# Down projection of a gated feed-forward: from nine pairs of row blocks by seven products and a plain rest to eleven pairs by seven products

## The chip, the cores and the metric

One NeuronCore of a Trainium2 chip runs the whole kernel. The time is device microseconds of one execution, as the median of several runs; the profile is one more execution of the same program. TensorE (PE) multiplies, VectorE (DVE), ScalarE (ACT) and GpSimd (POOL) work on the results, and SyncE (SP) and ScalarE issue transfers (queue names SPq, ACTq).

## The reference

One decoder layer on 512 tokens of 1024 channels, float32. First comes a mixer (a matrix-memory head group and a convolution group) with a residual, then a gated feed-forward with a causal convolution of width 3 over the tokens. The change concerns the feed-forward alone:

```python
D_FF = ((8 * D_MODEL // 3 + 127) // 128) * 128      # 2816 = 22 blocks of 128
...
u = rms_norm(x, ffn_pre_g[l]) * (1.0 + sc2) + sh2
up = causal_dwconv(u @ ffn_up[l], ffn_conv_w[l], ffn_conv_b[l])
a, gt = jnp.split(up, 2, axis=-1)
f = (jax.nn.silu(gt) * a) @ ffn_down[l]
x = x + g2 * rms_norm(f, ffn_post_g[l])
```

## The kernel before

**Products of split numbers.** A float32 operand is split in two parts, `hi` (a copy in the TensorE's rounded format, made on ScalarE) and `lo` (the rest, by a subtraction on VectorE or GpSimd). `mm3` multiplies a pair of operands by three matmuls: hi by hi, hi by lo, lo by hi. `w_split` makes the two parts of a weight piece, `w_load` loads a megabyte of weights through SP and splits it in four.

**The up stage.** The loop `for i in range(NF)` goes over the 22 blocks of the hidden width. For block i TensorE computes 48 matmuls of 512 columns, 24 for the value half into one PSUM bank and 24 for the gate half into another (`mmbank`, a pool of four buffers, so that block i+2 writes the banks of block i). `conv3` reads each bank three times: ScalarE makes the first tap (L1027), VectorE adds two more (L1029). The results are `fa` and `fg`. ScalarE puts `fg` through silu in place (L1097); this instruction is the `anchor`. VectorE multiplies the two, by halves of 256 tokens: `fx` for the first half, `fr` for the second.

**The down stage by seven products.** Two neighbouring blocks make a pair. Of the product of hidden values and down weights, the token halves are the rows, the two blocks of the pair the inner halves and the two halves of 512 output channels the columns: a two by two product of blocks, which a scheme with sums of blocks does in seven products instead of eight. Its sums of hidden values (`fy`, `fq`) are made on GpSimd in the up stage at every odd block and split there, or sent to DRAM (`spill["s34"]`, `spill["a22"]`, through ScalarE's queue) and read back by `back` in the down stage. Its sums of weights are made in the up stage too, one pair at each block that the table `AT` lists: `weight_load` fetches the pair's four pieces `b` (256 KB each, through ScalarE's queue, put behind the last silu by `behind`), `weight_sums` does four subtractions (L1048 and L1050 on VectorE, L1049 and L1051 on GpSimd, in the order 1048, 1049, 1050, 1051, each after the one before), and `weight_store` sends the four results `spillt` to DRAM from ScalarE's queue, behind the silu of the block after the sums. In the down stage `product` fetches the weights of one of the seven products in pieces of `GJ` pairs through SP into a ring of four buffers, splits each pair's piece and does 6 matmuls per pair. The seven are p1, p2, p6, p5, p7, p3, p4 in this order. Eight PSUM banks (`banks`, four token tiles by two halves of the output channels) collect them; `keep` copies a finished sum out and `put` adds it into another bank.

**The rest and the end.** Nine pairs (blocks 0 to 17) go by seven products. Blocks 18 to 21 stay whole (`f`), and are multiplied by their weights `wd` plainly, token tile by token tile, 24 matmuls each. After each tile comes the end chain: the multiply by the gain into `fo` (L1205), squares of the bank summed on ScalarE (L678), the factor of the norm (`token_factor`, one small operation on VectorE, L683, and a power on GpSimd, L685), the last multiply with the residual `xr` added (L1210), and the output through SP (L1211).

**What sets the order.** TensorE's and SP's instructions run in the order in which the code is written. Those of VectorE, ScalarE and GpSimd are put in order by the compiler's list scheduler when the kernel is built; `behind` adds an edge to it. Each engine then works in order.

Of the kernel before, what the change touches and what calls it, by code (L numbers as in the profile page):

```python
# [17 lines left out]
P = 128  # L18
D = 1024
# [35 lines left out]
def decoder_layer(ctx, tc, w_glu0, x, c, adaT, vecs, w_glu, w_qko, w_v0, w_v, w_out, w_up, w_down, out):  # L55
# [32 lines left out]
    def slot(name, dt=F32):  # L88
        return slots.tile([P, T], dt, tag="t", name=name)
# [108 lines left out]
    def mm3(ps, a, b, start, stop, again=False):  # L198

        for i, (l, r) in enumerate(((a[0], b[0]), (a[0], b[1]), (a[1], b[0]))):  # L200
            PE.matmul(ps, l, r, start=start and i == 0, stop=stop and i == 2, skip_group_check=again)  # L201
# [471 lines left out]
    def cvtile(name):  # L673
        return cvs.tile([P, T], F32, tag="cvs", name=name)

    def sq_sum(src, col, name):
        junk = small.tile([P, T], BF16, tag="junk", bufs=1, name=f"{name}junk")
        S.activation(junk, src, AF.Square, accum_out=col)  # L678

    def token_factor(sq, name):  # L680

        t = small.tile([P, 1], F32, tag="tt", name=f"{name}t")
        V.tensor_scalar(out=t, in0=sq[:, :1], scalar1=sq[:, 1:2], scalar2=D * EPS, op0=ALU.add, op1=ALU.add)  # L683
        r = small.tile([P, 1], F32, tag="tr", name=f"{name}r")
        G.tensor_tensor(out=r, in0=t, in1=mhalf[:, :1], op=ALU.pow)  # L685
        return r
# [342 lines left out]
            V.scalar_tensor_tensor(out=t[:, d:], in0=ps[:, : T - d], scalar=w(2 - d), in1=t[:, d:], op0=ALU.mult, op1=ALU.add)  # L1029
        return t  # L1030

    JP = 9
    NP = 2 * JP
    GJ = 3
    AT = [6, 7, 8, 10, 11, 12, 14, 15, 16]

    spill = {q: dram.tile([P, JP * T], F32, tag=f"spill{q}", name=f"spill{q}") for q in ("t1", "t2", "t3", "t4", "s34", "a22")}
    sums = {}
# [15 lines left out]
        for q, t in zip(("t1", "t3", "t4", "t2"), sums.pop(j)):  # L1054
            behind(nc.scalar.dma_start(spill[q][:, j * T : (j + 1) * T], t), anchor[0])

    f = {}
# [12 lines left out]

    for i in range(NF):
        if i < NE:
            pa, pg = early[i]
        else:
            pieces = w_load(w_up[i], f"wup{i}")
            if i in AT:
                weight_load(AT.index(i))
            if i in (4, 8, 12, 16):
                ada_block(38 + i // 2, last_lo[0])
                ada_block(39 + i // 2, last_lo[0])  # L1080
            if i == 19:
# [12 lines left out]
            pa, pg = both  # L1094
        a = conv3(pa, i, f"fa{i}")
        g = conv3(pg, NF + i, f"fg{i}")
        anchor[0] = S.activation(g, g, AF.Silu)  # L1097
        if i >= NP:
            V.tensor_tensor(out=a, in0=a, in1=g, op=ALU.mult)
            f[i] = split_f(a, f"f{i}", False)  # L1100
        else:
            if i % 2 == 0:
                x_, r_ = slot(f"fx{i}"), slot(f"fr{i}")
            cs = slice(i % 2 * HT, (i % 2 + 1) * HT)
            V.tensor_tensor(out=x_[:, cs], in0=a[:, :HT], in1=g[:, :HT], op=ALU.mult)
            V.tensor_tensor(out=r_[:, cs], in0=a[:, HT:], in1=g[:, HT:], op=ALU.mult)
            if i % 2:
                y_, q_ = slot(f"fy{i}"), slot(f"fq{i}")
                G.tensor_tensor(out=y_[:, :HT], in0=r_[:, :HT], in1=r_[:, HT:], op=ALU.add)
                G.tensor_tensor(out=y_[:, HT:], in0=y_[:, :HT], in1=x_[:, :HT], op=ALU.subtract)  # L1110
                G.tensor_tensor(out=q_[:, :HT], in0=x_[:, :HT], in1=r_[:, :HT], op=ALU.subtract)
                G.tensor_tensor(out=q_[:, HT:], in0=x_[:, HT:], in1=y_[:, HT:], op=ALU.subtract)
                af.append(split_f(x_, f"fx{i}", i == 1))
                asum.append(split_f(y_, f"fy{i}", i == 1))
                j = i // 2
                nc.scalar.dma_start(spill["s34"][:, j * T : (j + 1) * T], q_)
                nc.scalar.dma_start(spill["a22"][:, j * HT : (j + 1) * HT], r_[:, HT:])
# [11 lines left out]
    ring = [upool.tile([P, KT, T], F32, tag=tag, name=f"ring{tag}").rearrange("p j t -> p (j t)") for tag in ("uh", "ul")]  # L1129
    rings = [z[:, a : a + 2048] for a in (0, 2048) for z in ring]  # L1130

    def product(weights, left, th, hf, start, name):

        for a in range(0, JP, GJ):
            r = rings[at[0] % len(rings)] if at[0] > 1 else raws.tile([P, 2048], F32, tag="raw", name=f"{name}_{a}")
            at[0] += 1
            view = weights(a)
            nc.sync.dma_start(r[:, : GJ * T].rearrange("p (j n) -> p j n", j=GJ), view)
            for n in range(GJ):
                j = a + n  # L1140
                turn[0] += 1
                w = w_split(r[:, n * T : (n + 1) * T], f"{name}_{j}", eng=V if turn[0] % 2 else G)
                hi, lo, off = left(j)
                for q in range(2):
                    ts = slice(off + q * P, off + (q + 1) * P)
                    mm3(banks[2 * th + q][hf], (hi[:, ts], lo[:, ts]), w, start and j == 0, j == JP - 1, True)

    def plain(q):
        return lambda a: w_down[a : a + GJ, :, q * T : (q + 1) * T].rearrange("j p n -> p j n")

    def summed(q):
        return lambda a: spill[q][:, a * T : (a + GJ) * T].rearrange("p (j n) -> p j n", j=GJ)

    def keep(th, hf, name):
        out = [cvtile(f"{name}{q}") for q in range(2)]
# [17 lines left out]
    product(plain(0), lambda j: (*af[j], 0), 1, 1, True, "p1")  # L1173
    p1 = keep(1, 1, "kp1")
    product(plain(2), lambda j: (*af[j], HT), 0, 0, True, "p2")
    put(p1, 0, 0)
    product(summed("t2"), lambda j: (*asum[j], HT), 1, 1, False, "p6")
    u2 = keep(1, 1, "ku2")
    s34 = [back("s34", j * T, T, f"s34_{j}") for j in range(JP)]
    product(summed("t1"), lambda j: (*asum[j], 0), 0, 1, True, "p5")  # L1180
    p5 = keep(0, 1, "kp5")
    product(summed("t3"), lambda j: (*s34[j], 0), 1, 1, False, "p7")
    u3 = keep(1, 1, "ku3")
# [7 lines left out]
    wd = {}  # L1191
    for k in range(NP, NF, 2):
        pieces = w_load(w_down[k // 2], f"wd{k}")
        wd[k], wd[k + 1] = pieces[:2], pieces[2:]
    for tt in range(NT):
        for k in range(NP, NF):
            for hf in range(2):
                mm3(banks[tt][hf], (f[k][0][:, tok(tt)], f[k][1][:, tok(tt)]), wd[k][hf], False, k == NF - 1, True)
        res, xr = [], []
        for hf in range(2):  # L1200
            xr.append(cvtile(f"xr{tt}_{hf}"))
            nc.sync.dma_start(xr[hf], x1_d[tt][hf])
        for hf in range(2):
            m = slot(f"fo{tt}_{hf}")
            V.tensor_tensor(out=m, in0=banks[tt][hf], in1=g2r[hf], op=ALU.mult)  # L1205
# [3 lines left out]
        for hf in range(2):  # L1209
            V.scalar_tensor_tensor(out=res[hf], in0=res[hf], scalar=r, in1=xr[hf], op0=ALU.mult, op1=ALU.add)  # L1210
            nc.sync.dma_start(out[tok(tt), hf * T : (hf + 1) * T], res[hf])  # L1211


def _layout(i):
# [64 lines left out]
```

## Time and profile before

| | us |
|---|---|
| median of 3 runs (lowest, highest) | 780.26 (779.7, 780.34) |
| the profiled execution | 779.11 |
| its span | 777.3 |
| TensorE busy in the span | 763.5 (98%) |
| VectorE, GpSimd, ScalarE busy | 556.1, 510.9, 403.8 |
| mean granted TensorE clock | 0.998 of full speed |

The profiled execution is 1.8 us longer than its span, which runs from its first instruction to its last. In the profile's rows a time in us stands first where work is listed in order (its start, then its length), then engine, line, operation, what is written and read, and in brackets how long the engine sat idle before it and what ended that. Buffers carry the names of the program without their numbers. The up stage runs to 663 us (block 3 starts at 455 and each takes 10.9), the down stage from 663 to 770, and the end chain of the last tile after that.

### The profile page before, as it was taken

Reading aid. Unit: us, or ns where it says so; the run is one execution under the profiler, and the core shown is the slowest. Engines: PE = TensorE matmul, PEld = TensorE weight load, DVE = VectorE, ACT = ScalarE, POOL = GpSimd, SP = SyncE. Lnnn points to the kernel's source line nnn. Section 1 sums busy time; section 2 is a strip of 40 time slices with the busy share of each in tenths; the row PEclk is TensorE's granted clock in tenths of the full one; section 3 lists DMA queues with packets and bytes.
Section 4 is the critical chain, followed back from the end, with each engine's and each line's share of the span. In section 5 each row is a group of like instructions: output and inputs, shape, how many; then the busy total and the mean of one; then the engine's idle time right before and its main releaser. Section 6 shows DMA issues by size and latency. Waiting matters only on the chain.

```text
span 777.3 us, 10639 instructions
## 1 busy us (share of the span) xinstructions
PE 763.5 (98%) x3718; PEld 638.9 (82%) x3718; DVE 556.1 (72%) x817; ACT 403.8 (52%) x759; POOL 510.9 (66%) x422
## 2 busy tenths in 40 slices
PE   8999999999999999999999999999999999999996
PEld 6788898878888888878888998888888888888885
DVE  6669999979399496567868797566565666854544
ACT  6685538585657455471353554444344345646532
POOL 5789759796756544342751477787777983588860
PEclk9999999999999999999999999999999999999999
DMA  8963214214031161555953653557677663886715
GB/s 330 352 256 137 82 55 163 82 30 160 28 121 70 45 226 56 190 189 194 362 203 111 243 175 137 189 192 269 230 245 265 200 237 104 297 272 220 273 28 189
DMA packets 43897, 140.01 MB, mean 180 GB/s; under 512 B 4770, under 2 KB 6082, under 8 KB 37572
## 3 DMA queue, kind: packets, MB, share of 16 engines
q1 hardware_dynamic: 20772, 90.30, 32.7%
q10 hardware_dynamic: 23072, 49.04, 18.3%
q8 instruction: 29, 0.48, 0.3%
q14 instruction: 24, 0.20, 0.1%
HBM read 122.13 MB, written 17.19 MB: 179 GB/s over the span
## 4 chain that ended last, share of the span: by engine, by line
PE 78%; DVE 8%; DMA 4%; ACT 4%; issue 3%; POOL 1%; ACTq 0%; DVEq 0%; POOLq 0%
PE up L201 28%; PE dn L201 13%; PE qko L201 12%; PE glu L201 7%; PE v L201 6%; PE mixb L201 3%; PE o L530 2%; PE s L519 2%; PE mixa L201 2%; DMA spare<-in_adaT 2%; PE glu L347 2%; DVE cv L733 2%; DVE junk L167 1%; DMA wglu<-in_w_glu 1%; DMA ada<-in_adaT 1%
## 5 line engine op out<-in xcount | busy, mean ns | idle before, releaser
L733 DVE SCALAR_TENSOR_TENSOR cv<-gt,cvw,cv 128x488 f32<-128x488 f32 (+22 forms) x200 | 138.0, 729 | 2.9 <-ACT cv L721 1.3
L729 POOL TENSOR_TENSOR cs<-cs,cs 128x510 f32<-128x510 f32 (+3 forms) x32 | 41.7, 1304 | 0.1
L183 POOL TENSOR_TENSOR wup_1024l<-wup,wup_1024h 128x512 fp32r<-128x512 f32 x20 | 29.7, 1485 | 10.8 <-ACT wup_1024h L182 10.8
L201 PE MATMUL up<-u2h,wup_0h 128*128 128x512 f32 (+1 forms) x100 | 36.6, 366 | 0.2 <-DVE fa17c L1029 0.2
L201 PE MATMUL up<-u2l,wup_0h 128*128 128x512 f32 (+1 forms) x100 | 36.5, 365 | 0.2 <-DVE u2l L942 0.2
L201 PE MATMUL up<-u2h,wup_1024h 128*128 128x512 f32 (+1 forms) x100 | 36.4, 364 | 0.0
L201 PE MATMUL up<-u2h,wup_0l 128*128 128x512 f32 (+1 forms) x100 | 36.4, 364 | 0.0
L201 PE MATMUL up<-u2l,wup_512h 128*128 128x512 f32 (+1 forms) x100 | 36.4, 364 | 0.0
L201 PE MATMUL up<-u2h,wup_1536h 128*128 128x512 f32 (+1 forms) x100 | 36.4, 364 | 0.0
L201 PE MATMUL up<-u2h,wup_512h 128*128 128x512 f32 (+1 forms) x100 | 36.4, 364 | 0.0
L201 PE MATMUL up<-u2l,wup_1536h 128*128 128x512 f32 (+1 forms) x100 | 36.4, 364 | 0.0
L201 PE MATMUL up<-u2h,wup_1536l 128*128 128x512 f32 (+1 forms) x100 | 36.4, 364 | 0.0
L201 PE MATMUL up<-u2h,wup_512l 128*128 128x512 f32 (+1 forms) x100 | 36.4, 364 | 0.0
L201 PE MATMUL up<-u2h,wup_1024l 128*128 128x512 f32 (+1 forms) x100 | 36.4, 364 | 0.0
L201 PE MATMUL up<-u2l,wup_1024h 128*128 128x512 f32 (+1 forms) x100 | 36.3, 363 | 0.0
L167 DVE SCALAR_TENSOR_TENSOR junk<-ada,cb 128x1024 bf16<-128x1024 f32 x20 | 30.4, 1520 | 4.7 <-DMA ada<-in_adaT 4.6
L183 POOL TENSOR_TENSOR wup_0l<-wup,wup_0h 128x512 fp32r<-128x512 f32 x20 | 27.0, 1349 | 8.3 <-ACT wup_0h L182 8.2
L183 POOL TENSOR_TENSOR wup_1536l<-wup,wup_1536h 128x512 fp32r<-128x512 f32 x20 | 30.0, 1502 | 2.8 <-ACT wup_1536h L182 1.8
L183 POOL TENSOR_TENSOR wup_512l<-wup,wup_512h 128x512 fp32r<-128x512 f32 x20 | 28.5, 1426 | 4.5 <-ACT wup_512h L182 4.5
L727 ACT ACTIVATE cs<-gt,cvw 128x511 f32<-128x511 f32 (+4 forms) x40 | 27.1, 712 | 5.5 <-POOL cs L729 4.9
L1048 DVE TENSOR_TENSOR b<-b,b 128x512 f32<-128x512 f32 x9 | 13.9, 1543 | 21.9 <-DMA b<-in_w_down 21.9
L183 POOL TENSOR_TENSOR wqko_1024l<-wqko,wqko_1024h 128x512 fp32r<-128x512 f32 x12 | 15.5, 1290 | 16.3 <-PE v L201 9.1
(1049 smaller groups left out, 2744.6 us busy)
## 6 DMA issues: line engine op xcount, KB each, us to landing
wup<-in_w_up SPq DMA_DIRECT2D x22, 1024.0 KB, 4.8
wqko<-in_w_qko SPq DMA_DIRECT2D x12, 1024.0 KB, 4.7
ada<-in_adaT ACTq DMA_DIRECT2D x20, 512.0 KB, 4.6
b<-in_w_down ACTq DMA_DIRECT2D x36, 256.0 KB, 4.0
spillt<-b ACTq DMA_DIRECT2D x36, 256.0 KB, 3.3
ada<-in_adaT SPq DMA_DIRECT2D x16, 512.0 KB, 7.0
wo<-in_w_out SPq DMA_DIRECT2D x8, 1024.0 KB, 4.8
spare<-in_adaT ACTq DMA_DIRECT2D x12, 512.0 KB, 7.8
```

What stands on the lines that cost most here:

```text
L167: t = V.scalar_tensor_tensor(out=junk, in0=r, scalar=1.0, in1=cb, op0=ALU.mult, op1=ALU.mult, accum_out=mod[:, i : i + 1])
L183: (eng or G).tensor_tensor(out=lo[:, :n], in0=src, in1=hi[:, :n].bitcast(F32), op=ALU.subtract)
L201: PE.matmul(ps, l, r, start=start and i == 0, stop=stop and i == 2, skip_group_check=again)
L347: PE.matmul(ps, blk(wk, i)[a], u[k][b], start=k == 0 and p == 0, stop=k == KT - 1 and p == 1)
L519: PE.matmul(sp[:, :n], ks[d][:, cc * P : (cc + 1) * P], qs[d][:, cc * P :], start=d == 0, stop=d == 1)
L530: PE.matmul(o[:, : DH + 2], E[h][cc][:, a : a + P], vs[h][cc], start=cc == 0, stop=cc == tt)
L727: S.activation(t[:, d:], cvx[j][:, : T - d], AF.Copy, scale=w(CK - 1 - d))
L729: G.tensor_tensor(out=side[:, d:], in0=side[:, d:], in1=t[:, d:], op=ALU.add)
L733: tap = V.scalar_tensor_tensor(out=cp[:, d:], in0=cvx[j][:, : T - d], scalar=w(CK - 1 - d), in1=cp[:, d:], op0=ALU.mult, op1=ALU.add)
L1048: V.tensor_tensor(out=b11, in0=b12, in1=b11, op=ALU.subtract)
```

## The change

All eleven pairs go by the seven products (`JP = NF // 2`), so there is no plain rest; `AT` lists eleven blocks, and pieces of the products' weights hold four pairs (`GJ = 4`: 4, 4 and 3). Every block now makes `fx` and `fr`, every odd one the sums. The last product p4 is begun with pair 0 right after p7 (`p4a`), so that `put(u3)` can be done then; its pairs 7 to 10 are held back (`late`) and done tile by tile at the end, for token tiles 2 and 3. Tiles 0 and 1, and the other half of tiles 2 and 3, are finished or prepared before. At the end of a tile only one square is left, and the multiply by the gain is put behind the factor's first step.

ScalarE from the silu of block 8 to the first tap of block 9. The pieces `b` are the raw weights of a pair and, after the sums, the finished ones; `spillt` is DRAM; `wup` are up weights. Before:

```order
L1097 ACTIVATE fg8c<-fg8c 128x512
L1055 DMA spillt_4536<-b_0_4983 128x512
L1055 DMA spillt_4538<-b_1_4984 128x512
L1055 DMA spillt_4539<-b_2_4985 128x512
L1055 DMA spillt_4537<-b_3_4986 128x512
L182 ACTIVATE wup_1536h<-wup_5373 128x512
L1027 ACTIVATE fa9c<-up_0_5199,vec 128x512
```

and now:

```order
L1097 ACTIVATE fg8c<-fg8c 128x512
L1056 DMA spillt_4536<-b_0_5015 128x512
L1056 DMA spillt_4538<-b_1_5016 128x512
L1056 DMA spillt_4539<-b_2_5017 128x512
L1056 DMA spillt_4537<-b_3_5018 128x512
L1044 DMA b_0_5219<-in_w_down 128x512
L1044 DMA b_1_5220<-in_w_down 128x512
L1044 DMA b_2_5221<-in_w_down 128x512
L1044 DMA b_3_5222<-in_w_down 128x512
L1029 ACTIVATE fa9c<-up_0_5227,vec 128x512
```

Block 9 has sums now, and the loads for them have come in behind the four stores, ahead of the first tap.

VectorE from the taps of block 9 to its product. Before:

```order
L1029 SCALAR_TENSOR_TENSOR fa9c<-up_0_5199,vec,fa9c 128x511
L1050 TENSOR_TENSOR b_3_5097<-b_3_5097,b_0_5094 128x512
L1029 SCALAR_TENSOR_TENSOR fa9c<-up_0_5199,vec,fa9c 128x510
L1029 SCALAR_TENSOR_TENSOR fg9c<-up_1_5224,vec,fg9c 128x511
L1029 SCALAR_TENSOR_TENSOR fg9c<-up_1_5224,vec,fg9c 128x510
L1105 TENSOR_TENSOR fx_5169<-fa9c,fg9c 128x256
```

and now:

```order
L1031 SCALAR_TENSOR_TENSOR fa9c<-up_0_5227,vec,fa9c 128x511
L1031 SCALAR_TENSOR_TENSOR fa9c<-up_0_5227,vec,fa9c 128x510
L1049 TENSOR_TENSOR b_0_5219<-b_1_5220,b_0_5219 128x512
L1031 SCALAR_TENSOR_TENSOR fg9c<-up_1_5252,vec,fg9c 128x511
L1051 TENSOR_TENSOR b_3_5222<-b_3_5222,b_0_5219 128x512
L1031 SCALAR_TENSOR_TENSOR fg9c<-up_1_5252,vec,fg9c 128x510
L1101 TENSOR_TENSOR fx_5193<-fa9c,fg9c 128x256
```

The subtraction of block 8's sums that stood between the taps of `fa9` is gone, and both subtractions of block 9's stand between `fa9` and the last tap of `fg9`.

VectorE at the end of the last token tile (`ro3` is its factor, `dn` a bank). Before:

```order
L1205 TENSOR_TENSOR fo_0_7402<-dn_0_6442,g2r 128x512
L1205 TENSOR_TENSOR fo_1_7406<-dn_1_6436,g2r 128x512
L683 TENSOR_SCALAR ro3t<-fsq 128x1
L1210 SCALAR_TENSOR_TENSOR fo_0_7402<-fo_0_7402,ro3r,xr_0_7398 128x512
L1210 SCALAR_TENSOR_TENSOR fo_1_7406<-fo_1_7406,ro3r,xr_1_7400 128x512
```

and now:

```order
L685 TENSOR_SCALAR ro3t<-fsq 128x1
L1212 TENSOR_TENSOR fo_0_7495<-dn_0_6498,g2r 128x512
L1217 SCALAR_TENSOR_TENSOR fo_1_7451<-fo_1_7451,ro3r,xr_1_7447 128x512
L1217 SCALAR_TENSOR_TENSOR fo_0_7495<-fo_0_7495,ro3r,xr_0_7445 128x512
```

The multiply of half 0 has moved behind the factor's first step, that of half 1 far ahead, and half 1 is finished first.

Lines below L680 stand two further down in the changed code, so that silu is L1097 in both, the taps of VectorE L1031, the sums L1049 to L1052 and the stores L1056. The diff, with the parts left out that only rename or indent:

```diff
+    last_factor = [None]
+
     def token_factor(sq, name):
 
         t = small.tile([P, 1], F32, tag="tt", name=f"{name}t")
-        V.tensor_scalar(out=t, in0=sq[:, :1], scalar1=sq[:, 1:2], scalar2=D * EPS, op0=ALU.add, op1=ALU.add)
+        last_factor[0] = V.tensor_scalar(out=t, in0=sq[:, :1], scalar1=sq[:, 1:2], scalar2=D * EPS, op0=ALU.add, op1=ALU.add)
-    JP = 9
-    NP = 2 * JP
-    GJ = 3
-    AT = [6, 7, 8, 10, 11, 12, 14, 15, 16]
+    JP = NF // 2
+    GJ = 4
+    AT = [3, 5, 6, 7, 9, 10, 11, 13, 14, 15, 17]
-        if i >= NP:
-            V.tensor_tensor(out=a, in0=a, in1=g, op=ALU.mult)
-            f[i] = split_f(a, f"f{i}", False)
...
+        if i % 2 == 0:
+            x_, r_ = slot(f"fx{i}"), slot(f"fr{i}")
+        cs = slice(i % 2 * HT, (i % 2 + 1) * HT)
+        V.tensor_tensor(out=x_[:, cs], in0=a[:, :HT], in1=g[:, :HT], op=ALU.mult)
+        V.tensor_tensor(out=r_[:, cs], in0=a[:, HT:], in1=g[:, HT:], op=ALU.mult)
...
-    def product(weights, left, th, hf, start, name):
-
-        for a in range(0, JP, GJ):
+    def product(weights, left, th, hf, name, js=range(JP), start=False, by_tile=JP):
+
+        late = []
+        for a in range(js.start, js.stop, GJ):
+            m = min(GJ, js.stop - a)
             r = rings[at[0] % len(rings)] if at[0] > 1 else raws.tile([P, 2048], F32, tag="raw", name=f"{name}_{a}")
             at[0] += 1
-            view = weights(a)
-            nc.sync.dma_start(r[:, : GJ * T].rearrange("p (j n) -> p j n", j=GJ), view)
-            for n in range(GJ):
+            nc.sync.dma_start(r[:, : m * T].rearrange("p (j n) -> p j n", j=m), weights(a, a + m))
+            for n in range(m):
                 j = a + n
                 turn[0] += 1
                 w = w_split(r[:, n * T : (n + 1) * T], f"{name}_{j}", eng=V if turn[0] % 2 else G)
-                hi, lo, off = left(j)
-                for q in range(2):
-                    ts = slice(off + q * P, off + (q + 1) * P)
-                    mm3(banks[2 * th + q][hf], (hi[:, ts], lo[:, ts]), w, start and j == 0, j == JP - 1, True)
+                if j < by_tile:
+                    for q in range(2):
+                        piece(left(j), q, w, banks[2 * th + q][hf], start and j == 0, j == js.stop - 1)
+                else:
+                    late.append((j, w))
+        return late
+
+    def piece(left, q, w, ps, start, stop):
+        hi, lo, off = left
+        ts = slice(off + q * P, off + (q + 1) * P)
+        mm3(ps, (hi[:, ts], lo[:, ts]), w, start, stop, True)
...
+    a22 = [back_a22(0)]
+    product(summed("t3"), lambda j: (*s34[j], 0), 1, 1, "p7")
+    u3 = keep(1, 1, "ku3", slot)
     put(p5, 1, 1)
-    a22 = [back("a22", a * HT, min(T, (JP - a) * HT), f"a22_{a}") for a in range(0, JP, 2)]
-    product(plain(3), lambda j: (*s34[j], HT), 0, 1, False, "p3")
+    t4 = summed("t4")
+    product(t4, lambda j: (*a22[0], 0), 1, 0, "p4a", range(1), start=True)
+    put(u3, 1, 0)
+    a22 += [back_a22(a) for a in range(2, JP, 2)]
+    product(plain(3), lambda j: (*s34[j], HT), 0, 1, "p3")
     put(u2, 0, 1)
-    product(summed("t4"), lambda j: (*a22[j // 2], j % 2 * HT), 1, 0, True, "p4")
-    put(u3, 1, 0)
...
+    res, xr = {}, {}
...
+    def scaled(tt, hf):
+        res[tt, hf] = slot(f"fo{tt}_{hf}")
+        return V.tensor_tensor(out=res[tt, hf], in0=banks[tt][hf], in1=g2r[hf], op=ALU.mult)
+
+    def finish(tt, r):
+        for hf in (1, 0):
+            z = res[tt, hf]
+            V.scalar_tensor_tensor(out=z, in0=z, scalar=r, in1=xr[tt, hf], op0=ALU.mult, op1=ALU.add)
+            nc.sync.dma_start(out[tok(tt), hf * T : (hf + 1) * T], z)
...
+    late = product(t4, a22_left, 1, 0, "p4", range(1, JP), by_tile=JP - 4)
+    for tt in range(2):
+        x1_load(tt)
         for hf in range(2):
-            m = slot(f"fo{tt}_{hf}")
-            V.tensor_tensor(out=m, in0=banks[tt][hf], in1=g2r[hf], op=ALU.mult)
-            sq_sum(banks[tt][hf], fsq[:, 2 * tt + hf : 2 * tt + hf + 1], f"dn{tt}_{hf}")
-            res.append(m)
+            square(tt, hf)
+            scaled(tt, hf)
+        finish(tt, token_factor(fsq[:, 2 * tt : 2 * tt + 2], f"ro{tt}"))
+    for tt in range(2, NT):
+        x1_load(tt)
+        square(tt, 1)
+        scaled(tt, 1)
+    for tt in range(2, NT):
+        for j, w in late:
+            piece(a22_left(j), tt - 2, w, banks[tt][0], False, j == JP - 1)
+        square(tt, 0)
         r = token_factor(fsq[:, 2 * tt : 2 * tt + 2], f"ro{tt}")
-        for hf in range(2):
-            V.scalar_tensor_tensor(out=res[hf], in0=res[hf], scalar=r, in1=xr[hf], op0=ALU.mult, op1=ALU.add)
-            nc.sync.dma_start(out[tok(tt), hf * T : (hf + 1) * T], res[hf])
+        behind(scaled(tt, 0), last_factor[0])
+        finish(tt, r)
```

More of the change, by code (lines that the diff above doesn't have):

```diff
@@ L1171, in back, with back_a22 @@
         return hi, lo
-    product(plain(0), lambda j: (*af[j], 0), 1, 1, True, "p1")
+    def back_a22(a):
+        return back("a22", a * HT, min(T, (JP - a) * HT), f"a22_{a}")
+    product(plain(0), lambda j: (*af[j], 0), 1, 1, "p1", start=True)
     p1 = keep(1, 1, "kp1")
-    product(plain(2), lambda j: (*af[j], HT), 0, 0, True, "p2")
+    product(plain(2), lambda j: (*af[j], HT), 0, 0, "p2", start=True)
     put(p1, 0, 0)
-    product(summed("t2"), lambda j: (*asum[j], HT), 1, 1, False, "p6")
+    product(summed("t2"), lambda j: (*asum[j], HT), 1, 1, "p6")
@@ L1178, in decoder_layer @@
     u2 = keep(1, 1, "ku2")
     s34 = [back("s34", j * T, T, f"s34_{j}") for j in range(JP)]
-    product(summed("t1"), lambda j: (*asum[j], 0), 0, 1, True, "p5")
+    product(summed("t1"), lambda j: (*asum[j], 0), 0, 1, "p5", start=True)
     p5 = keep(0, 1, "kp5")
-    product(summed("t3"), lambda j: (*s34[j], 0), 1, 1, False, "p7")
-    u3 = keep(1, 1, "ku3")
+    a22 = [back_a22(0)]
+    product(summed("t3"), lambda j: (*s34[j], 0), 1, 1, "p7")
+    u3 = keep(1, 1, "ku3", slot)
     put(p5, 1, 1)
-    a22 = [back("a22", a * HT, min(T, (JP - a) * HT), f"a22_{a}") for a in range(0, JP, 2)]
@@ new lines, in scaled, with a22_left @@
+    def scaled(tt, hf):
[6 more added lines that the diff above has]
+            nc.sync.dma_start(out[tok(tt), hf * T : (hf + 1) * T], z)
+    def a22_left(j):
+        return *a22[j // 2], j % 2 * HT
+    late = product(t4, a22_left, 1, 0, "p4", range(1, JP), by_tile=JP - 4)
```

53 lines of the change are left out of this document (20 added, 33 removed).

## The prediction

> **What bounds the kernel now.** I read the page first, then what TensorE waits for from 430 us on, then the chain that ended last, then ScalarE, VectorE and the groups around the up stage.
>
> ```profile
> PE 763.5 (98%) x3718; PEld 638.9 (82%) x3718; DVE 556.1 (72%) x817; ACT 403.8 (52%) x759; POOL 510.9 (66%) x422
> ...
> PE up L201 <- DVE fa17c L1029: 0.2, 1, 0.2
> ...
> 628.88 0.67 DVE fa17c L1029
> ...
> 629.68 11.15 PE up L201 x48
> ...
> 640.94 21.81 PE up L201 x96
> 662.74 101.56 PE dn L201 x447
> ```
>
> The second row is the whole answer on TensorE's waits from 430 us to the end: one, of 0.2 us. So TensorE sets the time through both stages of the feed-forward. A matmul takes 21.81/96 = 0.2272 us there, a block of 48 takes 10.91, and in the down stage 101.56/447 is 0.2272 again. Less matmuls means less time, as long as TensorE stays fed. The one wait warns: block 19 started at 629.68 and not at 629.46, because VectorE had not finished `fa17c`, and block 19 writes the PSUM bank that block 17 still held. Of the four `mmbank` buffers a block takes two.
>
> So there is a limit. Call S the start of block i on TensorE: 629.46 - 10.91 per block before 19, so 454.9 for block 3, 476.8 for 5, 607.6 for 17. The gate half `fg` of block i is read out when its silu (L1097) starts. Its bank is wanted after two blocks and a half, at S + 27.3 us; that of `fa` at S + 21.8.
>
> ```profile
> 474.10 0.64 ACT L1097 ACTIVATE fg3c<-fg3c 128x512 f32<-128x512 f32 x1 [4.64 <-DVE fg3c L1029]
> ...
> 491.12 0.62 ACT L1097 ACTIVATE fg5c<-fg5c 128x512 f32<-128x512 f32 x1
> ...
> 529.09 0.63 ACT L1097 ACTIVATE fg8c<-fg8c 128x512 f32<-128x512 f32 x1 [2.94 <-DVE fg8c L1029]
> ...
> 536.25 0.63 ACT L1097 ACTIVATE fg9c<-fg9c 128x512 f32<-128x512 f32 x1 [1.52 <-DVE fg9c L1029]
> 550.38 0.63 ACT L1097 ACTIVATE fg10c<-fg10c 128x512 f32<-128x512 f32 x1 [3.01 <-DVE fg10c L1029]
> ...
> 562.36 0.63 ACT L1097 ACTIVATE fg11c<-fg11c 128x512 f32<-128x512 f32 x1 [5.36 <-DVE fg11c L1029]
> ...
> 575.84 0.63 ACT L1097 ACTIVATE fg12c<-fg12c 128x512 f32<-128x512 f32 x1 [2.94 <-DVE fg12c L1029]
> 575.86 2.05 ACTq L1055 DMA_DIRECT2D spillt<-b  x4
> ...
> 583.43 0.63 ACT L1097 ACTIVATE fg13c<-fg13c 128x512 f32<-128x512 f32 x1 [1.94 <-DVE fg13c L1029]
> ...
> 631.07 0.63 ACT L1097 ACTIVATE fg17c<-fg17c 128x512 f32<-128x512 f32 x1 [1.92 <-DVE fg17c L1029]
> 641.82 0.63 ACT L1097 ACTIVATE fg18c<-fg18c 128x512 f32<-128x512 f32 x1 [1.14 <-DVE fg18c L1029]
> ```
>
> Lag of the silu behind S: block 3 19.2 us, block 5 14.4, 9 15.9, 13 19.4, 17 23.4. From block 9 to 13 this loop takes 47.2 us, from 13 to 17 47.6; TensorE needs 43.6. The loop of convolution and sums runs slower than TensorE where sums are in it, and the slack is used up just at block 17, where the 0.2 us wait stands. Its steps: a block with sums takes 14.1 (9 to 10), 12.0 (10 to 11), 13.5 (11 to 12); one without 7.6 (12 to 13, odd) or 10.75 (17 to 18, even).
>
> **The change, part by part.** *Matmuls.* Before: 7 products x 9 pairs x 6 = 378, and 4 blocks x 2 halves x 4 tiles x 3 = 96. After: 7 x 11 x 6 = 462. Twelve less, -12 x 0.2272 = -2.73 us, all on TensorE's path.
>
> *Two more sums in the up stage.* Eleven pairs instead of nine: 8 loads, 8 stores and 8 subtractions more.
>
> ```profile
> L1048 DVE TENSOR_TENSOR b<-b,b 128x512 f32<-128x512 f32 x9 | 13.9, 1543 | 21.9 <-DMA b<-in_w_down 21.9
> ...
> L1049 POOL TENSOR_TENSOR b<-b,b 128x512 f32<-128x512 f32 x9 | 11.6, 1293 | 15.3 <-DVE fr L1106 8.9 <-DMA b<-in_w_down 3.0 <-PE up L201 2.7
> L1050 DVE TENSOR_TENSOR b<-b,b 128x512 f32<-128x512 f32 x9 | 11.0, 1220 | 8.7 <-POOL b L1049 8.7
> ...
> b<-in_w_down ACTq DMA_DIRECT2D x36, 256.0 KB, 4.0
> spillt<-b ACTq DMA_DIRECT2D x36, 256.0 KB, 3.3
> ...
> DMA to landing us min/median/max: 2.7/3.8/5.3
> ...
> 503.54 1.78 ACTq L1043 DMA_DIRECT2D b<-in_w_down  x4
> ...
> 556.04 1.61 DVE L1048 TENSOR_TENSOR b<-b,b 128x512 f32<-128x512 f32 x1 [1.56 <-DMA b<-in_w_down]
> 557.57 1.52 DVE L1029 SCALAR_TENSOR_TENSOR fa11c<-up,vec,fa11c 128x511 f32<-128x511 f32 x2
> 559.06 1.77 DVE L1050 TENSOR_TENSOR b<-b,b 128x512 f32<-128x512 f32 x1
> 560.75 1.52 DVE L1029 SCALAR_TENSOR_TENSOR fg11c<-up,vec,fg11c 128x511 f32<-128x511 f32 x2
> ```
>
> A sum costs more than its busy time because the loads wait for the silu before (`behind`), VectorE waits for them in order (21.9 us over nine), and the next silu stands behind that. After block 5 the new order repeats in fours, 6-7-8-9, and every one of the sums at 7, 9, 11, 13, 15 has the 4 stores of the pair before, or of an older one, ahead of its loads on ScalarE's queue. Step by step, silu to silu:
> - Odd, first (8 to 9): 2.05 for the four stores, 0.9 for the first two loads (1.78 for four), 4.0 to landing = 7.0 (before, without stores, L1048 starts 5.7 after silu 10, so up to 7.7). Then L1048 1.54, POOL's 1.29, which writes over what L1048 read, L1050 1.22, the last `fg` tap 0.76, and 0.2 between: 12.0. Nearest row: 10 to 11, 12.0.
> - Even with sums (9 to 10): between the rows 14.1 and 13.5, but L1050 now comes after the silu; I take 13.7, low end 14.1 - 1.22 = 12.9.
> - Odd, third (10 to 11): 7.0 + 1.54 + two taps 1.5 = 10.1; high end the row 12.0.
> - Even without (11 to 12): 10.75 and the L1050 left over, 1.2: 11.9; low end 10.75.
>
> Together 47.7 (45.3 to 50, the ends of the steps added), 4.1 more than TensorE. The start is later too: block 3's sum puts its silu 1.5 later at least (a L1048 ahead of it), block 4 keeps its step of 9.4 to 9.8, and 4 to 5 is 12.0 where it was 7.2. So silu 5 at about 497.0, lag 20.2 instead of 14.4. Lag at 9: 24.3; 13: 28.4; 17: 32.5. The limit is 27.3, so TensorE stalls 5.1 us in all: 1.1 for block 13's bank, 2.8 for 14's, the rest up to 17's. Worked with `fa` and 21.8 I get 5.0. After 17 there are no sums and the lag falls by 3.9 per pair.
>
> What of it hides: SP's queue holds the weights of the next blocks and no b load, so nothing of SP's is late. POOL has 4 subtractions more and the products' `fy`, `fq` of blocks 18 to 21; it is the fullest after VectorE, but nobody in the row of TensorE's waits waited for it. The halves of 18 to 21 replace one product and one split each by two and two; beside 21.8 us per pair without sums I price it at 0.
>
> *The start of the down stage.*
>
> ```profile
> 663.59 1.53 DVE L1029 SCALAR_TENSOR_TENSOR fg21c<-up,vec,fg21c 128x511 f32<-128x511 f32 x2 [0.53 <-ACT fg21c L1027]
> ```
>
> Before, block 21 came out 2.4 us after the up stage's last matmul, and its factors were wanted 90 us later. Now p1's last pair wants them, 60 x 0.2272 = 13.6 us after that matmul. With the lag at its limit at 17 and falling, silu 21 comes about 9 us behind it, and two products, a copy and a subtraction 5.4 us later: 0.8 us late (0 where the lag is as before, 2 where it does not fall).
>
> *Down stage.* Six weight splits more in about 102 us, pieces of four on SP. ScalarE and POOL read back `s34`:
>
> ```profile
> 712.78 0.63 ACT L1169 ACTIVATE s_7h<-s_7r 128x512 fp32r<-128x512 f32 x1 [2.39 <-DMA s_7r<-spills]
> ...
> 717.13 0.63 ACT L1169 ACTIVATE s_8h<-s_8r 128x512 fp32r<-128x512 f32 x1 [1.01 <-DMA s_8r<-spills]
> ...
> 660.00:765.00 105.00, 105.00 (x464) 86.77 (x463) 56.99 (x56) 53.77 (x100) 73.97 (x52) 1.00 0.63 217
> ```
>
> One comes each 4.35 us, three pairs of p7 take 4.1. Eleven instead of nine start earlier in the products that went before, which are two pairs longer each; that is their cover. By my placing, s34 of pair 9 has 1 to 3 us to spare. 0, up to +2. The window (TensorE, weight loads, VectorE, ScalarE, POOL in that order) shows VectorE and ScalarE half idle, POOL at 70%. The early pair of p4 and the moved `put(u3)` change no count; 0.
>
> *The end.*
>
> ```profile
> 769.76 1.37 DVE L1205 TENSOR_TENSOR fo<-dn,g2r 128x512 f32<-128x512 f32 x2 [0.92 <-PE dn L201]
> 770.02 0.39 PE L201 MATMUL dn<-wd_1536h,f21l 128*128 128x512 f32 x1
> 771.27 0.60 ACT L678 ACTIVATE dn_1junk<-dn 128x512 bf16<-128x512 f32 x1
> 772.28 0.55 POOL L685 TENSOR_TENSOR ro3r<-ro3t,mhalf 128x1 f32<-128x1 f32 x1 [4.89 <-DVE ro3t L683]
> 772.87 1.42 DVE L1210 SCALAR_TENSOR_TENSOR fo<-fo,ro3r,xr 128x512 f32<-128x512 f32 x2 [0.66 <-POOL ro3r L685]
> 765.00:778.00 13.00, 5.41 (x24) 4.13 (x22) 5.33 (x10) 2.75 (x8) 1.10 (x2) 0.85 0.48 162
> ```
>
> Before, the second square starts 771.27 - 770.41 = 0.86 us after the last matmul, behind `fo`. After, the only square follows the matmul; with 0.06 for that, -0.80. The `fo` multiply (1.37/2 = 0.69) lies beside POOL's 0.55 and its way there and back; if it does not fit, 0.1 to 0.2 comes back. From the factor on both are alike.
>
> **Sum.** The profiled run took 779.11 (span 777.3 and 1.8 outside). 779.11 - 2.73 - 0.80 + 5.1 + 0.8 = 781.5. The median 780.26 lies 1.15 above that run, so 782.6.
>
> **Rivals.** *No stall, the other side.* The loop's place is the same; it decides at a lag of 27.3 at block 17, which is a group of 46.0 us or less with the start I took. Nothing is then late, and 779.11 - 3.53 + 1.15 = 776.7. For it: even with sums by its low end 12.9, even without 10.75; against it: rows of 47.2 and 47.6 with the same three sums in four.
>
> *A small stall.* A group of 46.6 to 47.2 puts the lag at 29 to 31, a stall of 2 to 4 with the gain of 3.53 against it: about 779 to 781.5, no change.
>
> *Loads queue behind stores.* A store moves as much as a load, and ahead of five more loads now stand four stores. If loads landed in 5.3 instead of 4.0 us (the slowest, by the answer on `b` above), six odd steps give 7.8 us: 790. Against it: the step 11 to 12 had stores and loads behind one silu too, and is shorter (13.5) than 9 to 10 (14.1) without stores. The Trainium skill, page "DMA: Bandwidth & Descriptors", section "Issuing engines are not separate DMA queues", says that transfers of all issuers run on the same 16 engines and interleave; by that the loads share time with the stores instead of standing behind them, and the sum stays. The two steps agree.
>
> *The clock falls.* In the last window the granted clock is 0.85 over 13 us: full for 9.1 us, half after, so it fell at 774.1, 3.7 us after the last matmul. A stall of 3.7 us in one piece would so bring a stretch at half speed; if that is as long as the stall it costs another 1.8: 784.4. My pieces are 1.1, 2.8 and 1.2, so it needs two joined. The Trainium skill, page "TensorE: Matmul & The Clock Gate", section "What's actually happening", gives a window of about 3.4 us idle for the fall and as much busy for the return; the 3.7 agrees.
>
> **How the numbers follow.** Chances: the forecast (a stall of 5 to 10 with the late p1) 0.40, no stall 0.30, a small one 0.18, queueing loads 0.07, the clock 0.05. A difference under 0.2% (1.6 us, so 778.7 to 781.8) can't be told from no change: faster 0.30, same 0.18, slower 0.52. The forecast alone has 781.8 to 786; with the groups' ends 45.3 and 50 the stall lies between 0 and about 12, so the range reaches from 776.4, the floor with a little more from the end, to 789.0.
>
> **What would show it.** Among TensorE's waits: `up` for `fa` and `fg` of blocks 13 to 17, 5 us in all, and about 1 us of `dn` for `fx21l`. Silu starts at 9, 13 and 17 that lie 47.7 apart; right if within 0.7. The down stage: 462 matmuls in 105 us. At the end: the square at once behind the last matmul. Wrong if the lag at 17 is under 27, or if the down stage waits for `s34`, `a22` or a weight split.

## The result, and the profile after

The changed kernel takes 789.39 us (median of 5 runs, 787.77 to 790.79) against 780.26: 1.0117 times the kernel before, 95% interval 1.0101 to 1.0132. It is slower, as forecast, but by 9.1 us and not 2.4, and so a little beyond the stated range, which ended at 789.0.

The profiled execution took 789.39 as well, its span 787.5, 10.2 more than before (the profiled execution before lay 1.15 below its median, this one on it). From the page, TensorE's busy time and matmuls, and then all that TensorE waits for from 430 us on (in total, times, longest):

```profile
PE 763.6 (97%) x3706; PEld 636.6 (81%) x3706; DVE 566.8 (72%) x832; ACT 408.4 (52%) x768; POOL 527.4 (67%) x436
...
PE up L201 <- DVE fg14c L1031: 1.6, 1, 1.6
PE up L201 <- DVE fa15c L1031: 1.2, 1, 1.2
PE up L201 <- DVE fa12c L1031: 1.1, 1, 1.1
PE up L201 <- DVE fa13c L1031: 1.1, 1, 1.1
PE up L201 <- DVE fa11c L1031: 0.6, 1, 0.6
PE up L201 <- DVE fa16c L1031: 0.5, 1, 0.5
PE up L201 <- DVE fa14c L1031: 0.4, 1, 0.4
PE up L201 <- DVE fa18c L1031: 0.3, 1, 0.3
PE up L201 <- DVE fg13c L1031: 0.2, 1, 0.2
```

Twelve matmuls less, as counted. Before there was one wait of 0.2 us; now nine banks come late, those of blocks 11 to 18, 7.0 us in all, 5.2 of them for `fa` banks. There is no wait in the down stage. The rows count only what the profile ascribes to a releaser; the block starts show the whole. The first matmul of block 3, before:

```profile
455.22 0.40 PE L201 MATMUL up<-u2h,wup_0h 128*128 128x512 f32 x1
```

and after:

```profile
456.13 0.40 PE L201 MATMUL up<-u2h,wup_0h 128*128 128x512 f32 x1
```

That is 0.9 us from the stages before, which the change does not touch. Block 19 starts 9.3 us later than before and the up stage ends 9.8 later, so 8.9 us were lost between.

The loop that falls behind, by the silus on ScalarE:

```profile
496.89 0.63 ACT L1097 ACTIVATE fg5c<-fg5c 128x512 f32<-128x512 f32 x1 [4.77 <-DVE fg5c L1031]
...
546.05 0.63 ACT L1097 ACTIVATE fg9c<-fg9c 128x512 f32<-128x512 f32 x1 [4.87 <-DVE fg9c L1031]
...
595.99 0.63 ACT L1097 ACTIVATE fg13c<-fg13c 128x512 f32<-128x512 f32 x1 [4.84 <-DVE fg13c L1031]
...
644.33 0.63 ACT L1097 ACTIVATE fg17c<-fg17c 128x512 f32<-128x512 f32 x1 [4.86 <-DVE fg17c L1031]
```

The groups of four take 49.2, 49.9 and 48.3 us, where TensorE needs 43.6.

The end of the kernel (start, length; SPq is SyncE's queue of transfers):

```profile
770.81 1.00 SPq L1218 DMA_DIRECT2D out<-fo  x2
...
771.86 0.95 SPq L1205 DMA_DIRECT2D xr<-x1d  x2
...
774.96 1.42 DVE L1217 SCALAR_TENSOR_TENSOR fo<-fo,ro1r,xr 128x512 f32<-128x512 f32 x2 [2.32 <-DMA xr<-x1d]
...
776.40 0.81 SPq L1218 DMA_DIRECT2D out<-fo  x2
...
777.06 0.39 PE L201 MATMUL dn<-p_10h,a_10l 128*128 128x512 f32 x1
777.26 1.92 SPq L1205 DMA_DIRECT2D xr<-x1d  x4
777.55 0.60 ACT L678 ACTIVATE dn_0junk<-dn 128x512 bf16<-128x512 f32 x1 [2.03 <-PE dn L201]
...
780.31 0.75 DVE L1217 SCALAR_TENSOR_TENSOR fo<-fo,ro2r,xr 128x512 f32<-128x512 f32 x1 [3.22 <-DMA xr<-x1d]
...
782.90 1.41 DVE L1217 SCALAR_TENSOR_TENSOR fo<-fo,ro3r,xr 128x512 f32<-128x512 f32 x2
```

The square does follow the last matmul (ends 777.45) at once. But the residual tiles `xr` of token tiles 2 and 3 stand on SyncE's queue behind the outputs of tile 1, those behind tile 1's last multiply, and that waits for tile 1's own `xr`, issued behind the outputs of tile 0. So the last `xr` go out from 777.26 on and VectorE waits 3.2 us for them; the last multiply stands 5.45 us after the last matmul, where it was 2.46 (770.41 to 772.87). Before the change the loads stood behind the outputs of the tile before, too:

```profile
769.26 0.95 SPq L1202 DMA_DIRECT2D xr<-x1d  x2
```

But there the last one was out 1.15 us before the last matmul ended, and the last multiply waited for the factor from GpSimd and not for it.

Put together: 0.9 (ahead of block 3) + 8.9 (up stage) - 2.7 (matmuls) + 3.0 (end) = 10.1 of the 10.2 us of the span.

### The profile page after: what moved, and what is told of

The parts are those of the page before. It is cut to its first block, busy times and chain, and to the rows that moved or that the text cites. A ratio compares the mean times of both kernels' runs of the same rounds, so it can differ in the third digit from the quotient of the medians.

```text
span 787.5 us, 10699 instructions
## 1 busy us (share of the span) xinstructions
PE 763.6 (97%) x3706; PEld 636.6 (81%) x3706; DVE 566.8 (72%) x832; ACT 408.4 (52%) x768; POOL 527.4 (67%) x436
## 3 DMA queue, kind: packets, MB, share of 16 engines
q1 hardware_dynamic: 21396, 91.87, 32.6%
## 5 line engine op out<-in xcount | busy, mean ns | idle before, releaser
L183 POOL TENSOR_TENSOR wup_1536l<-wup,wup_1536h 128x512 fp32r<-128x512 f32 x20 | 28.3, 1416 | 22.1 <-ACT wup_1536h L182 21.7
L183 POOL TENSOR_TENSOR wup_1024l<-wup,wup_1024h 128x512 fp32r<-128x512 f32 x20 | 27.2, 1359 | 9.4 <-ACT wup_1024h L182 9.4
L201 PEld LDWEIGHTS up<-u2h,wup_0h 128*128 128x128 f32 x100 | 18.9, 189 | 10.5 <-ACT wup_512h L182 4.0
```

Of the source, the lines that this page charges most:

```text
L183: (eng or G).tensor_tensor(out=lo[:, :n], in0=src, in1=hi[:, :n].bitcast(F32), op=ALU.subtract)
```

## The experiments

Times are medians, with the ratio to the kernel before, run on the same chip, and its 95% interval in brackets. The traces are each of one execution, and where that one lies far from the median it is said.

**The residual tiles loaded ahead.**

```diff
-            xr[tt, hf] = cvtile(f"xr{tt}_{hf}")
+            xr[tt, hf] = slot(f"xr{tt}_{hf}")
...
-    for tt in range(2):
-        x1_load(tt)
+    for tt in range(NT):
+        x1_load(tt)
+    for tt in range(2):
...
     for tt in range(2, NT):
-        x1_load(tt)
```

> The changed kernel, with the residual tiles xr of all four token tiles kept in the pool of slots and loaded in one go, ahead of tile 0's end chain (they were loaded tile by tile, behind the outputs of the tile before on SyncE's queue). Theory: the end of the changed kernel waits on that queue (xr of tiles 2 and 3 issued at 777.26, landed 780.3, last multiply 782.9, 5.45 us after the last matmul). Then the last multiply follows the last matmul by about 1.7 us and 3.5 to 4 us go: 785.5, with the up stage's waits of 8.9 us unchanged. Rival: the end is long because VectorE and ScalarE have several tiles' work there; then under 1 us goes.

789.18 us, 1.0117 (1.0054 to 1.0179): the time can't be told from the changed kernel's, and 785.5 had been expected. In the profile the waits for `xr` are gone, and the end is shorter, but not by what was expected; TensorE lost 9.7 us in the up stage of this run.

```profile
768.99 0.42 ACT L1173 ACTIVATE a_10h<-a_10r 128x256 fp32r<-128x256 f32 x1 [1.47 <-DMA a_10r<-spilla]
...
778.54 0.39 PE L201 MATMUL dn<-p_10h,a_10l 128*128 128x512 f32 x1
...
779.86 1.42 DVE L1217 SCALAR_TENSOR_TENSOR fo<-fo,ro2r,xr 128x512 f32<-128x512 f32 x2
...
782.06 1.41 DVE L1217 SCALAR_TENSOR_TENSOR fo<-fo,ro3r,xr 128x512 f32<-128x512 f32 x2
```

The last multiply comes 3.1 us after the last matmul. The last read-back of `a22` is copied at 768.99, 9.5 us before the last matmul starts; in the changed kernel it was at 764.43, 12.6 before. So the splits of the last weight pieces, behind it on ScalarE, came later, and VectorE had them and several tiles' ends to do at once: from 769.96 to its last multiply it has no pause. That the new loads held up the read-backs is likely, but not shown by this run alone.

**The same, but later, and without new buffers for tiles 0 and 1.**

```diff
-    def x1_load(tt):
+    def x1_load(tt, make=cvtile):
...
-            xr[tt, hf] = cvtile(f"xr{tt}_{hf}")
+            xr[tt, hf] = make(f"xr{tt}_{hf}")
...
-    for tt in range(2):
-        x1_load(tt)
+    for tt in range(NT):
+        x1_load(tt, cvtile if tt < 2 else slot)
+    for tt in range(2):
...
     for tt in range(2, NT):
-        x1_load(tt)
```

> The changed kernel with the residual tiles issued together ahead of tile 0's end chain, but tiles 0 and 1 in the four buffers they had and only tiles 2 and 3 in slots, so that the loads wait for the last put and do not run beside the read-backs of a22. Theory: in the run with all loads ahead the last multiply still came 3.1 us after the last matmul because those loads delayed a22 and with it p4's splits and VectorE's work at the end; here it comes 1.7 to 2.2 us after it, 3 to 3.7 less than the 5.45 of the changed kernel, and TensorE's waits in the up stage stay at 8 to 10 us. Time 785 to 786.5. Rival: VectorE's work of four tiles is what fills the end; then it stays at 3 us and above.

786.46 us, 1.0063 (1.0043 to 1.0083); the interval lies under the changed kernel's. The profiled execution was the fastest of its six (782.25, the others 786.4 to 788.0): it started block 3 at 454.16, 2.0 us earlier than the changed kernel's, and lost 7.5 us in the up stage, a little under the 8 to 10 expected. Its end does not hang on that. The last matmul ends at 774.12:

```profile
774.22 0.60 ACT L678 ACTIVATE dn_0junk<-dn 128x512 bf16<-128x512 f32 x1 [2.03 <-PE dn L201]
...
775.82 1.41 DVE L1217 SCALAR_TENSOR_TENSOR fo<-fo,ro3r,xr 128x512 f32<-128x512 f32 x2
```

1.70 us after it, 3.75 less than in the changed kernel and 0.8 less than before. The end chain itself gives what was forecast of it, and the late residual loads were the rest. The rival, VectorE's work, falls. What the run does not separate is the place on the queue from the buffers: tiles 2 and 3 got buffers of their own as well, and in the old four, tile 3's load could not have gone before tile 1's last multiply (774.96 to 776.38 in the changed kernel).

**The first subtraction of the sums behind the silu.**

```diff
-        V.tensor_tensor(out=b11, in0=b12, in1=b11, op=ALU.subtract)
+        behind(V.tensor_tensor(out=b11, in0=b12, in1=b11, op=ALU.subtract), anchor[0])
```

> The changed kernel, with the first subtraction of each pair's weight sums (L1049) put behind the silu of the same block, so that it does not stand ahead of the gate half's taps on VectorE. Theory: TensorE's 8.9 us of waits in the up stage come from the taps standing behind that subtraction and its loads, which itself wait for the stores to free their buffers. Then an odd block with sums takes about 9 us from silu to silu and not 12.8, a group of four about 43 and not 49 to 50, and TensorE waits under 1.5 us: about 781. Rival: it is the loads' issue on ScalarE's queue ahead of the value half's tap, or the work itself; then the steps lose under 1 us each and 785 or more is left.

778.73 us, 0.9979 (0.996 to 0.9998), against 1.0117 for the changed kernel (about 781 had been expected), and TensorE has no wait at all from 430 us on. The step from block 8 to 9 in the changed kernel, on ScalarE and VectorE:

```profile
533.26 1.96 ACTq L1056 DMA_DIRECT2D spillt<-b  x4
535.27 2.34 ACTq L1044 DMA_DIRECT2D b<-in_w_down  x4
537.65 0.78 ACT L1029 ACTIVATE fa9c<-up,vec 128x512 f32<-128x512 f32 x1 [3.77 <-DMA spillt<-b]
...
540.60 1.53 DVE L1049 TENSOR_TENSOR b<-b,b 128x512 f32<-128x512 f32 x1 [0.60 <-DMA b<-in_w_down]
542.05 0.74 DVE L1031 SCALAR_TENSOR_TENSOR fg9c<-up,vec,fg9c 128x511 f32<-128x511 f32 x1
543.53 1.76 DVE L1051 TENSOR_TENSOR b<-b,b 128x512 f32<-128x512 f32 x1 [0.74 <-POOL b L1050]
545.22 0.74 DVE L1031 SCALAR_TENSOR_TENSOR fg9c<-up,vec,fg9c 128x510 f32<-128x510 f32 x1
```

and with the subtraction behind the silu:

```profile
533.15 0.78 ACT L1029 ACTIVATE fa9c<-up,vec 128x512 f32<-128x512 f32 x1 [3.93 <-DMA spillt<-b]
...
536.19 1.53 DVE L1031 SCALAR_TENSOR_TENSOR fg9c<-up,vec,fg9c 128x511 f32<-128x511 f32 x2 [0.69 <-ACT fg9c L1029]
537.64 1.23 DVE L1049 TENSOR_TENSOR b<-b,b 128x512 f32<-128x512 f32 x1
```

The stores and loads on ScalarE's queue hold its tap back in both (4.4 and 4.5 us after silu 8). What goes are the subtractions and their wait from between the taps: silu to silu 9.2 us instead of 12.8, the groups of four 44.6, 45.0 and 45.2 instead of 48 to 50. (`behind` sets the order when the kernel is built; on the chip VectorE does not wait for the silu, which starts at 537.82, 0.18 after the subtraction.) That is more than the 43 expected and more than TensorE's 43.6, but from a lag of 15.0 at block 5 it does not reach the limit by block 17.

**Nine sums only.** `AT` as before the change, the summed products' last two pairs read earlier sums.

```diff
-    AT = [3, 5, 6, 7, 9, 10, 11, 13, 14, 15, 17]
+    AT = [6, 7, 8, 10, 11, 12, 14, 15, 16]
...
+            first = min(a, len(AT) - (b - a))
+            return spill[q][:, first * T : (first + b - a) * T].rearrange("p (j n) -> p j n", j=b - a)
```

> The changed kernel with weight sums for nine pairs only, at the blocks where the kernel before had them; the four summed products take the sums of earlier pairs for the last two, so those sums are left out of the computation. All else is as changed (fx, fr and sums of hidden values in all blocks, 462 matmuls, the end). Theory: two more sums and their places make the waits; TensorE waits then at most 1 us in the up stage and the time falls by 8 to 9 us, to about 781. Rival: the waits come from the rest of the change; then it stays above 786.

779.77 us, 1.0009 (0.9985 to 1.0033), for a kernel that no longer computes the layer. No wait of TensorE either. So the waits come from the two sums and their places, not from the new products of hidden values or GpSimd's share of blocks 18 to 21. And it is not faster than before although it has twelve matmuls less: the last matmul ends at 767.74 there, 2.7 us earlier than before, and the last multiply comes 4.6 us after it and not 2.46.

**Eleven sums in the old rhythm.**

```diff
-    AT = [3, 5, 6, 7, 9, 10, 11, 13, 14, 15, 17]
+    AT = [3, 4, 6, 7, 8, 10, 11, 12, 14, 15, 16]
```

> The changed kernel with eleven sums at blocks 3, 4, 6, 7, 8, 10, 11, 12, 14, 15, 16: the rhythm of before (blocks 9, 13 and 17 without), with the two more ones early. It tells number from place. If number decides, each sum costs the loop 3.5 to 4 us, the silu of block 17 lags by about the same 35 us and the waits stay at 7 to 9 us: 788 to 789. If place decides (a sum in the odd block after a silu behind which four stores stand ahead of the loads), a group of four takes 47.2 to 47.6 us as before, the lag at 17 is 28 to 31 and the waits are 1 to 4 us: 782 to 785.

784.99 us (runs from 781.1 to 789.27), 1.0052 (1.002 to 1.0083). Place and number both count. The groups take 46.1, 47.6 and 47.5 us, near those of before (45.1, 47.2 and 47.6); the place makes the other 3.1, 2.3 and 0.8 of the changed kernel's groups. But silu 5 lags by 18.2 us instead of 14.1 (from the block starts in the traces) and silu 16 by 32.6, 5.3 over the limit, and 5.0 us are lost in waits, more than the 1 to 4 expected if place decided alone. Another 1.6 us went in the profiled execution in another way, told below. That execution took 788.83 and is among the slowest of ten, so the waits of the median one can be shorter.

**Only the second subtraction moved.** At blocks 3, 7, 11, 15, behind the product `fr`.

```diff
-        V.tensor_tensor(out=b22, in0=b22, in1=b11, op=ALU.subtract)
+        second = V.tensor_tensor(out=b22, in0=b22, in1=b11, op=ALU.subtract)
+        if AT[j] % 4 == 3:
+            behind(second, product_r[0])
...
-        V.tensor_tensor(out=r_[:, cs], in0=a[:, HT:], in1=g[:, HT:], op=ALU.mult)
+        product_r[0] = V.tensor_tensor(out=r_[:, cs], in0=a[:, HT:], in1=g[:, HT:], op=ALU.mult)
```

> The changed kernel with the second subtraction on VectorE (L1051) of the sums at blocks 3, 7, 11 and 15 alone put behind the products fx and fr of the same block; the first stays ahead of the gate half's taps. Theory: the step from such a block to the next one without sums took 12.85, 12.84 and 11.9 us, where the prediction had 11.9, because that subtraction (1.8 us and 1.0 us of waiting for GpSimd) stands ahead of fx and fr, GpSimd's sums of hidden values start late, and the spill of fq on ScalarE's queue, which waits for them, stands ahead of the gate half's first tap. Without it these steps take 10.7 to 11.2, the lag at 17 falls by 4 to 6 us and TensorE's waits from 8.9 to 3 to 5 us: about 784 to 785.5. Rival: the spill waits for GpSimd's other work anyway; then the steps stay above 12 and the time at 788 to 789.

> The changed kernel once more, beside the run before this one: 788 to 790, TensorE's waits in the up stage 8 to 10 us, the last multiply 5.4 us after the last matmul.

791.6 us, 1.0129 (1.0083 to 1.0175), and the changed kernel beside it 791.3, 1.0133 (1.0088 to 1.0178): on this chip 1.3 us above the 788 to 790 expected, but with a ratio that agrees with the first one, 9.5 us lost in the up stage and a last multiply 5.85 us after the last matmul. The steps from 7 to 8, 11 to 12 and 15 to 16 take 12.6, 12.6 and 12.1 us: the theory falls. The rival holds for the steps, though its time of 788 to 789 was passed. From the run with the subtraction moved (its traced execution, 787.93, was the fastest of four), GpSimd and ScalarE after silu 7 (518.93):

```profile
523.82 1.29 POOL L1054 TENSOR_TENSOR b<-b,b 128x512 f32<-128x512 f32 x1
525.07 0.73 POOL L1108 TENSOR_TENSOR fy<-fy,fx 128x256 f32<-128x256 f32 x1
525.77 1.29 POOL L183 TENSOR_TENSOR wup_1536l<-wup,wup_1536h 128x512 fp32r<-128x512 f32 x1
527.01 1.18 POOL L1110 TENSOR_TENSOR fq<-fx,fy 128x256 f32<-128x256 f32 x1
...
528.23 0.33 ACTq L1114 DMA_DIRECT2D spills<-fq  x1
...
529.14 0.76 ACT L1029 ACTIVATE fg8c<-up,vec 128x512 f32<-128x512 f32 x1
```

`fx` and `fr` were earlier, but GpSimd does the sums' last subtraction and a weight split in between without a pause, `fq` is ready at 528.2, 9.3 us after the silu where it was 9.5 in the changed kernel, and its spill stands ahead of the gate half's tap on ScalarE. This step is bound by GpSimd and by the spill's place on ScalarE's queue.

**Both mendings, and the sums' order alone in the kernel before.**

> Both mendings: the sums' first subtraction behind the silu, and the residual tiles as in the run before this one. If the two costs are separate they add: no waits of TensorE in the up stage and a last multiply 1.7 to 2.2 us after the last matmul, 778.7 - 2 = 776 to 777, 0.4 to 0.5% under the kernel before, which is the floor of the prediction (776.7). If the end is bound otherwise, it stays at 778 to 779.

775.92 us, 0.9939 (0.9917 to 0.9962): 0.6% under the kernel before, and no wait of TensorE.

```profile
766.89 0.39 PE L201 MATMUL dn<-p_10h,a_10l 128*128 128x512 f32 x1
...
768.97 1.41 DVE L1217 SCALAR_TENSOR_TENSOR fo<-fo,ro3r,xr 128x512 f32<-128x512 f32 x2
```

Block 3 starts at 455.27 here, as before, so the two traces can be laid side by side: the last multiply starts 3.9 us before that of the kernel before (772.87), 2.7 from the twelve matmuls, 0.8 from the end and 0.4 from the up stage. The prediction's floor had the first two as 3.53.

> The kernel before, with the first subtraction of its nine sums put behind the silu in the same way. Theory: the loop's speed costs nothing as long as the lag stays under the limit, so only the one wait of 0.2 us can go: no difference (within 0.2%), though the lag of silu 17 falls from 23 us to 12 or less. Rival: the order of the sums is worth time by itself, also where TensorE did not wait; then it is 1 us or more faster.

779.66 us, 0.9985 (0.997 to 1.0001). Its silu 17 lags by 17.7 us instead of 23.4 (12 was expected), and it is no faster that can be told. In the kernel before the loop's pace cost at most the one wait; the gain of the version above is the change's own, set free.

## Why the prediction was right and wrong

**The limit was right.** The lag rule gives 35.9 us at block 17 after the change (644.33 less 608.48, the unstalled start) against 27.3: 8.6 us over, and 8.9 were lost. It also gives the 5 us of the old rhythm, and none for the four kernels without waits, whose lags reach 25.1 at most. The silu's lag stands in for both halves, though: most of the waits were for `fa`, whose limit of 21.8 is met earlier in the block, as in the one wait before the change, at a silu lag of 23.4.

**The start of the loop was right by luck.** Silu 5 was put at 497.0 and came at 496.89, but errors cancelled on the way. Block 3's sum was to make silu 3 1.5 us later, at 475.6; it came at 473.85, though the whole stage started 0.9 later. The steps from 3 to 4 and from 4 to 5 then took 10.6 and 12.4, where 9.4 to 9.8 and 12.0 were taken. By the rule's own measure the lag was 19.0 and not 20.2.

**The pace of the loop was mis-sized.** This is the first step that failed: a group of 47.7 us, where 49.2, 49.9 and 48.3 were measured. From 5 to 9 the steps were 12.1 (even with sums; 13.7 taken), 11.4 (odd, third; 10.1), 12.9 (even without; 11.9) and 12.8 (odd, first; 12.0). The odd, third one came 1.3 us longer, on the way to the row that had been named as its high end (12.0):

```profile
511.16 2.30 ACTq L1044 DMA_DIRECT2D b<-in_w_down  x4
...
517.57 1.29 DVE L1049 TENSOR_TENSOR b<-b,b 128x512 f32<-128x512 f32 x1 [1.69 <-DMA b<-in_w_down]
```

The first subtraction starts 6.4 us after the first load goes out, where 0.9 + 4.0 had been taken. In the odd, first one the same stretch is 5.3 us, and the second subtraction took 1.76 where the mean before was 1.22. In the even one without sums the term was the 1.2 us of a left-over subtraction, which is not what binds it. So the stall was 8.9 us and not 5.1, inside the 0 to 12 that the steps' ends allowed. (The low ends of the steps add up to 45.75 and not to 45.3, which changes nothing here.)

**The end was wrong in sign.** This is the second step that failed, and the range had no room for it: -0.80 was forecast, +3.0 came. The prediction followed VectorE, ScalarE and GpSimd to the last multiply and did not follow SyncE's queue there, so the wait for `xr` stood in it at nothing. Before, tiles ended 5.45 us apart, so that each tile's outputs, and the `xr` loads behind them, were out before the next tile's last matmul ended. Now tiles 0 and 1 end together, their factors begun some 8 us before the last matmul, tile 1's residual load stands behind tile 0's outputs, and those of tiles 2 and 3 behind tile 1's outputs, which wait for tile 1's load. The run with the loads ahead of the outputs gives -0.76, near the forecast term.

**p1's wait did not come.** 0.8 us had been put in for the factors of block 21. After block 17 the loop caught up faster: silu 21 stands 6.2 us behind the last matmul of the up stage, not 9.

**The account.** The forecast was 6.8 us short. The stall makes 3.8 of it, the end 3.8 and the stages before block 3 0.9; p1's wait (0.8) and the 1.15 between profiled run and median were added and did not come. About 0.2 stays unassigned.

**Rivals.** No stall, and a small one of 2 to 4 us, on the changed kernel: refused by nine waits and 8.9 us lost. Loads queueing behind stores gave about the measured time (790), and its premise came true in part. Median times from issue to landing of a `b` load are 4.0 us before; in the changed kernel and in the run with the subtraction behind the silu they are

```profile
b<-in_w_down ACTq DMA_DIRECT2D x44, 256.0 KB, 4.9
```

```profile
b<-in_w_down ACTq DMA_DIRECT2D x44, 256.0 KB, 5.2
```

So later loads are part of the longer steps. But they landed later still in the second of these kernels, and there TensorE waits for nothing: a late load costs only because taps stand behind the subtraction that waits for it. And the end, of which that rival says nothing, makes 3 of the 9 us. The clock: no piece of the changed kernel's waits was long enough, as forecast; for the limit, see below.

## What to carry to other kernels

A loop that runs beside TensorE cost nothing here until its lag reached what the buffers allow; so work the lag out block by block, and bound the pace by the slowest like row, since an error of 1.5 us per group comes back once per group. What stands between two steps of such a loop in program order, and waits for another engine or a queue, is worth moving behind them, even when its own work gets no shorter. At the end of a kernel follow every queue of transfers, not only the arithmetic: a load that stands behind an output waits for all that the output waits for.

## What was not expected of the hardware

In the run with the old rhythm TensorE stood idle for 2.4 us in one piece, behind `fg16c`, and then ran at half speed. TensorE's wait, then stretches of that run, with the granted clock third from the end:

```profile
PE up L201 <- DVE fg16c L1031: 2.2, 1, 2.2
...
629.00:632.00 3.00, 0.77 (x5) 0.33 (x3) 2.74 (x3) 0.08 (x1) 2.50 (x2) 1.00 0.96 382
632.00:633.00 1.00, 1.00 (x4) 0.87 (x5) 0.42 (x2) 0.55 (x1) 0.00 (x0) 0.90 0.85 326
633.00:636.00 3.00, 3.00 (x8) 2.30 (x7) 1.21 (x4) 2.20 (x4) 2.21 (x2) 0.50 0.89 336
636.00:639.00 3.00, 3.00 (x14) 2.44 (x13) 2.93 (x4) 1.32 (x3) 2.37 (x3) 0.96 0.49 147
```

The gap ends at 631.97. By the granted clock of the last three rows, 0.2, 3.0 and 0.2 us ran at half speed, 3.4 together, from 632.8 on, when matmuls had run again for 0.8 us. In that stretch they stand 0.43 us apart instead of 0.227, and 1.6 us are lost by their starts. In the changed kernel a gap of 1.8 us (ahead of the gate half of block 16) had no such sequel. The prediction took 3.7 us as the least gap that does it; in this one execution the fall came behind a shorter one, 2.4. The Trainium skill, page "TensorE: Matmul & The Clock Gate", section "What's actually happening", names one idle window of about 3.4 us and that the window runs free. The 3.4 us at half speed agree; a fall behind 2.4 us of idling does not. What decides between gaps of 1.8 and 2.4 stays open, since no run here varied them.
